# Seven-product blocks over six k-tiles, and a down projection in three parts, in a decoder layer on one core

## The chip, the core and the metric

The kernel runs on one core of one Trainium2 chip. The metric is the device time of one execution in microseconds (us), taken as the median of several. The engines are named as in the profile: PE does the matmuls (PEld the loading of its stationary operand), ACT and DVE the elementwise work, POOL a few small operations, and SP issues nearly all DMAs.

## The reference

One layer for 256 tokens of width 2048, all in float32:

```
x = x + 0.5 * SwiGLU_1(rmsnorm(x))          # D_FF = 5632
x = x + mixer(rmsnorm(x))                   # w_in: 2048 -> 11776, attention and a gated MLP, two merges, w_out
x = x + 0.5 * SwiGLU_2(rmsnorm(x))
out = rmsnorm(x)
swiglu(x) = (silu(x @ w_gate) * (x @ w_up)) @ w_down
```

Nearly all of the work is products of 256 tokens with large weights, which are read once from memory.

## The kernel before

**Products.** A weight is taken in columns of 512 (a "gemm" of the program) and in k-tiles of 128 rows. Both operands are split into a high and a low part; a k-tile's product is three matmuls per 128 tokens (high by high, high by low, low by high), so 6 for the 256 tokens. The activations are the stationary operand, the weights stream through as 512 columns.

**Steps.** The list of steps sets the order of nearly everything (lay_out, lines 118 to 150). An "n" step is two k-tiles of one gemm, 12 matmuls. `ends` holds the position of a step's end in units of an n step. Work that follows a gemm (activation, transposition, residual) is put on a list of callbacks by such a position and is issued when the loop over steps gets there (lines 1112 to 1123).

**Quads.** In most pairs of neighbouring gemms, four k-tiles (two pairs) are multiplied as 2 x 2 blocks in Strassen's way: with blocks b11, b21, b12, b22 of the weights (k-tile of a pair by gemm) seven products p1 to p7 take the place of eight. Each is an "s" step, 2 x 3 = 6 matmuls, half a unit long. DVE forms the differences of weights first (prepare, line 222: t1 = b12 - b11, t3 = b12 - b22, t2 = b22 - t1, t4 = b21 - t2); the sums of the activations are made once per input (sums_of, line 319). ACT copies partial results between banks after p1, p6 and p7 (lines 306 to 311); DVE does so after p7 and p5 (lines 313, 315). OPEN and CLOSE say where the s steps stand: p1, p6, p7 before the last 5, 3 and 1 steps of the pair before, p5, p3, p2, p4 after the first 1, 3, 4, 5 of their own.

**Splits.** Every step's weights pass through split (line 235): ACT copies to the high part (wh, line 249), DVE subtracts it to get the low part (wl, line 250). There are four buffers of two k-tiles for each (LA = 3, so LA + 1). A step's split is issued four steps ahead, right after the products of the step that used the same buffer (advance, line 1087).

**Memory traffic.** Plain weights come in units of four k-tiles of 1 MB into three buffers (load_unit, line 167). The blocks of a quad come from load_block (line 211), 512 KB each, into a "home"; the next quad's block is asked for as soon as the split has read the old one (FREES, line 231). All this is issued on SP in program order.

**FFN.** Its hidden width is 11 columns of 512 (f = 0 to 10). Two halves: gate and up for f = 0 to 5, then the down product of these 24 k-tiles for four column groups c, added to x (residual, line 435); then f = 6 to 10 and 20 k-tiles. After up, DVE multiplies gate and up (line 507), transposes in 32 x 32 blocks, a DMA out and four back finish the transposition (turn, line 355), and ev splits the result into the h tiles (line 512). Quads of the kernel before: 13 in the first FFN, 15 in the second, 6 in the mixer.

Of the kernel before, what the change touches and what calls it, by code (L numbers as in the profile page):

```python
# [37 lines left out]
LA = 3  # L38
CS = (2, 0, 0)
CM = 2  # L40
RAWB = 3
# [4 lines left out]
def layer(ctx: ExitStack, tc: tile.TileContext, a, out):  # L46
# [63 lines left out]
    def gemm(w, c0, rows0, nk, lhs, post, group=(1, None), bank=None, quad=None):  # L110
        gemms.append(dict(w=w, c0=c0, rows0=rows0, nk=nk, lhs=lhs, post=post, group=group, bank=bank or mm_bank,
                          quad=quad, steps=0, begun=[False] * NT, left=[3 * nk] * NT))


    OPEN = ((5, "p1"), (3, "p6"), (1, "p7"))
    CLOSE = ((1, "p5"), (3, "p3"), (4, "p2"), (5, "p4"))

    def lay_out():
        i = 0
        while i < len(gemms):  # L120
            g = gemms[i]
            size, stage = g["group"]
            chunk = g["quad"] and g["quad"]["chunk"]
            order = [(p, q) for p in range(size) for q in range(gemms[i + p]["nk"] // 2)
                     if not g["quad"] or q // 2 != chunk]
# [3 lines left out]
            if g["quad"]:  # L129
                quad = g["quad"]  # L130
                quad["gemms"] = gemms[i], gemms[i + 1]
                for k, form in OPEN:
                    steps.insert(len(steps) - k, ("s", (quad, form)))
                for k, form in reversed(CLOSE):
                    new.insert(k, ("s", (quad, form)))
                quads.append(quad)
                for h in quad["gemms"]:
                    h["left"] = [3 * (h["nk"] - 4) + 6] * NT
                gemms[i + 1]["left"][1] += 18
            steps.extend(new)  # L140
            i += size
        t = -1.0
        for kind, s in steps:
            t += 1 if kind == "n" else 0.5
            ends.append(t)
            if kind == "n":
                hus.append(s)
                s[0]["steps"] += 1
            else:
                s[0]["gemms"][s[1] in ("p3", "p5", "p6", "p7", "p1")]["steps"] += 1  # L150

# [15 lines left out]
    def load_unit(i, parts=(0, 4)):  # L167
        if i not in raws and RAWB <= i < 2 * RAWB:
            if i == RAWB:
                raws["more"] = big.tile([P, RAWB * UK, NC], F32, tag="A", name="more")  # L170
            raws[i] = raws["more"][:, (i - RAWB) * UK:(i - RAWB + 1) * UK]
# [23 lines left out]
    def gate_home():  # L195
        b_ = big.tile([P, 6, 2, NC], F32, tag="B", name="quads")
        return [b_[:, b] for b in range(6)] + [big.tile([P, NC], F32, tag="k2", name="part")]

    def merge_home():
        l_ = sb.tile([P, 3, 2, NC], F32, tag="L", name="quads")  # L200
        k = big.tile([P, 2, NC], F32, tag="k2", name="quads4")
        w = sb.tile([P, 3, NC], F32, tag="W", name="part")
        t = sb.tile([P, 2, NC], F32, tag="tmp", bufs=2, name="sum")
        return [l_[:, b] for b in range(3)] + [k, t, w[:, 1:3], w[:, 0]]

    def move_in(home):
        home["room"] = home["make"]()
# [3 lines left out]
    def load_block(quad, b):  # L211
        if quad is None:
            return
        g, j = quad["gemms"][b // 2], b % 2
        k0 = g["rows0"] + 4 * quad["chunk"] * P
        src = g["w"][k0:k0 + 4 * P, g["c0"]:g["c0"] + NC].rearrange("(q j p) c -> p j q c", p=P, j=2)
        SP.dma_start(blocks_of(quad)[b], src[:, j])

    def blocks_of(quad):
        return quad["home"]["room"]  # L220
# [10 lines left out]
    FREES = {"p1": 0, "p2": 1, "p7": 2, "p3": 3}  # L231

    place = {}

    def split(i, k=slice(0, 2)):
# [8 lines left out]
        if i not in splits:  # L244
            wh = big.tile([P, 2, NC], F32R, tag="wh", bufs=LA + 1, name=f"wh{i}")
            wl = big.tile([P, 2, NC], F32R, tag="wl", bufs=LA + 1, name=f"wl{i}")
            splits[i] = (wh, wl)
        wh, wl = splits[i]
# [6 lines left out]
    def product(g, t, act, w, last=False):  # L255
# [10 lines left out]
    def products(i, ts=range(NT), jjs=range(2), high_first=False):  # L266
# [10 lines left out]
        for jj in jjs:  # L277
            k = u * UK + 2 * j + jj
# [8 lines left out]
    def quad_products(i, quad, form):  # L287
# [6 lines left out]
        k = 4 * quad["chunk"]  # L294
        for q in range(2):
            if form in ("p1", "p2", "p4"):
                kk, tt = {"p1": (0, 0), "p2": (1, 0), "p4": (1, 1)}[form]
                hi, lo = (v[:, k + 2 * q + kk, tt * P:(tt + 1) * P] for v in first["lhs"]())
            else:
                hi, lo = (v[:, ("p5", "p6", "p7", "p3").index(form), q] for v in quad["forms"]())  # L300
            for act, w in ((hi, wh), (hi, wl), (lo, wh)):
                product(g, t, act, w[:, q], q == 1 and act is lo)
# [16 lines left out]
    def sums_of(i, store, v, name, tag="gate"):  # L319
# [3 lines left out]
        def sums():  # L323
            w = v.rearrange("p (q m) i b -> p m q i b", m=4)
            a0, a1, b0, b1 = (w[:, m] for m in range(4))
            got["f"] = f = sb.tile([P, 4, 2, P], F32, tag=tag, bufs=2, name=f"fs{name}")
# [6 lines left out]
        def parts():  # L333
            both = store()
            split_psum(both[:, 0], both[:, 1], got["f"])
# [4 lines left out]
    def forms_tile(pool, tag, name, keep):  # L340
        def store():
            keep["forms"] = pool.tile([P, 2, 4, 2, P], F32R, tag=tag, name=name)
            return keep["forms"]
        return store

    def forms_in(keep):
        return lambda: (keep["forms"][:, 0], keep["forms"][:, 1])
# [51 lines left out]
    def norm_open(n):  # L399
        xT["hi"] = big.tile([P, KD, S], F32R, tag="xhi", name=f"xhi{n}")  # L400
# [54 lines left out]
    def turn_x(i, n, c, lag, read=3):  # L455
        def evac(src):
# [4 lines left out]
            split_psum(hi, lo, src)  # L461
            if c == CS[n]:
                sums_of(i + lag, forms_tile(big, "oT", f"fx{n}", xT), src, f"x{n}")
# [7 lines left out]
    merge = dict(make=merge_home)  # L471

    def ffn(wg, wu, wd, down_post, group):
        halves = ((0, 6), (6, 11))
        home = dict(make=ffn_home)
        homes.append(home)
        for hf, (f0, f1) in enumerate(halves):
            st = {}

            def lhs_x():  # L480
                return xT["hi"], xT["lo"]

            def lhs_h(st=st):
                return st["hi"], st["lo"]

            for f in range(f0, f1):
# [10 lines left out]
                def post_up(e, banks, st=st, f=f, f0=f0):  # L497
                    sg = st["sg"]
                    kl = 4 * (f - f0)
                    if f == f0:  # L500
                        st["hi"] = big.tile([P, 24, S], F32R, tag="A", name=f"hhi{e}")
                        st["lo"] = big.tile([P, 24, S], F32R, tag="B", name=f"hlo{e}")
# [7 lines left out]
                    def ev(src):  # L510
                        hi, lo = st["hi"][:, kl:kl + 4], st["lo"][:, kl:kl + 4]
                        split_psum(turned(hi), turned(lo), src)
                        if f == f0:
                            sums_of(e + 10, forms_tile(sb, "L", f"fh{e}", st), src, f"h{e}")

                    at(e + 1, mul)
                    turn(e + 2, f"h{e}", 8, put_tokens(lambda: sg), lambda: flat(sg), ev)
# [8 lines left out]
                quad = dict(chunk=CS[n], forms=forms_in(xT), home=home if f or not n else merge)  # L526
                gemm(wg, f * NC, 0, KD, lhs_x, post_gate, BOTH if f else PAIR, bank, quad)
                gemm(wu, f * NC, 0, KD, lhs_x, post_up, BOTH, bank, quad)
            for c in range(4):
                if c % 2 == 0:  # L530
                    bank = side()
                    quad = dict(chunk=0, forms=forms_in(st), home=home)
                gemm(wd, c * NC, f0 * NC, 4 * (f1 - f0), lhs_h,
                     lambda e, banks, c=c, hf=hf: down_post(e, c, banks, hf == 1), PAIR if c == 0 else BOTH,
                     bank, quad)
# [60 lines left out]
    def post_gelu(key, j):  # L596
        def post(e, banks):
            if j == 0 and key == "vs":
                    uv = big.tile([P, 2, NT, SGW], F32, tag="A", name="uv")
                    mix["vs"], mix["u"] = uv[:, 0], uv[:, 1]  # L600
# [577 lines left out]
```

## Time and profile before

| | |
|---|---|
| median of 3 runs | 2014.4 us (2014.35 to 2016.39) |
| profiled execution: its own time | 2016.67 us |
| profiled execution: span from first to last instruction | 2014.9 us |
| mean granted PE clock | 0.998 |
| matmuls of products of weights (line 257) | 9108 of 9281 PE instructions |
| splits on DVE and on ACT (lines 250, 249), 128x1024 | 875 each |
| DMA | 471.54 MB, mean 234 GB/s |

The profile is one execution. A row of a group of instructions reads: line, engine, operation, tiles written <- read, shape written <- read, count, busy time in us, mean of one in ns, and idle time of that engine just before them with what ended it. In the order of time a row is start in us, duration in us, engine and instruction; [..] is the idle time before and its releaser. Matmuls overlap: one takes 0.38 us from start to end, but they start closer together than that.

### The profile page before, as it was taken

Reading aid. Unit: us, or ns where it says so; the run is one execution under the profiler, and the core shown is the slowest. Engines: PE = TensorE matmul, PEld = TensorE weight load, DVE = VectorE, ACT = ScalarE, POOL = GpSimd, SP = SyncE. Lnnn points to the kernel's source line nnn. Section 1 sums busy time; section 2 is a strip of 40 time slices with the busy share of each in tenths; the row PEclk is TensorE's granted clock in tenths of the full one; section 3 lists DMA queues with packets and bytes.
Section 4 is the critical chain, followed back from the end, with each engine's and each line's share of the span. In section 5 each row is a group of like instructions: output and inputs, shape, how many; then the busy total and the mean of one; then the engine's idle time right before and its main releaser. Section 6 shows DMA issues by size and latency. Waiting matters only on the chain.

```text
span 2014.9 us, 24165 instructions
## 1 busy us (share of the span) xinstructions
PE 1996.0 (99%) x9281; PEld 1741.1 (86%) x9281; DVE 1505.2 (75%) x1536; ACT 1141.1 (57%) x1286; POOL 11.2 (1%) x19
## 2 busy tenths in 40 slices
PE   9999999999999999999999999999999999999998
PEld 8888888888888888888888888878888888888887
DVE  6787866788877688675665777788878776787775
ACT  6556554555556566454554555566655554566554
POOL 0000000000000000000000000000000000000000
PEclk9999999999999999999999999999999999999999
DMA  9877776667775985888877666678777766677764
GB/s 314 271 246 243 232 238 204 209 217 236 247 245 167 317 272 169 240 287 251 262 244 239 225 202 224 222 245 255 228 234 241 243 208 201 220 243 230 233 214 143
DMA packets 249723, 471.54 MB, mean 234 GB/s; under 512 B 12684, under 2 KB 41224, under 8 KB 249480
## 3 DMA queue, kind: packets, MB, share of 16 engines
q1 hardware_dynamic: 249288, 469.47, 71.9%
q8 instruction: 72, 1.18, 0.2%
q10 hardware_dynamic: 320, 0.53, 0.1%
q14 instruction: 43, 0.35, 0.1%
HBM read 440.30 MB, written 29.66 MB: 233 GB/s over the span
## 4 chain that ended last, share of the span: by engine, by line
PE 87%; DMA 5%; DVE 4%; ACT 2%; issue 2%; SPq 1%; POOLq 0%; POOL 0%; ACTq 0%; DVEq 0%
PE qd L257 67%; PE mm L257 18%; DMA xt<-bmx 2%; DVE wl L250 2%; ACT wh L249 1%; DMA bmx<-btx 1%; DMA uroom<-bmu 1%; ACT xt L459 1%; DMA raw<-in_w_in_dram 1%; DMA p<-bmp 1%; SPq L368 1%; DVE btx L378 0%; ACT junk L406 0%; ACT xhi L350 0%; DVE xlo L351 0%
## 5 line engine op out<-in xcount | busy, mean ns | idle before, releaser
L250 DVE TENSOR_TENSOR wl<-raw,wh 128x1024 fp32r<-128x1024 f32 (+1 forms) x637 | 772.4, 1217 | 313.3 <-ACT wh L249 311.6
L249 ACT ACTIVATE wh<-raw 128x1024 fp32r<-128x1024 f32 (+1 forms) x637 | 666.5, 1051 | 503.7 <-PE qd L257 314.6
L257 PE MATMUL qd<-wl,xhi 128*128 128x512 f32 x1296 | 491.4, 379 | 0.7 <-DVE wl L250 0.7
L257 PE MATMUL qd<-wh,xhi 128*128 128x512 f32 x1296 | 491.2, 379 | 0.0
L257 PE MATMUL qd<-wh,xlo 128*128 128x512 f32 x1296 | 491.2, 379 | 0.0
L257 PEld LDWEIGHTS qd<-wl,xhi 128*128 128x128 f32 x1296 | 244.9, 189 | 36.3 <-DVE wl L250 1.6
L257 PEld LDWEIGHTS qd<-wh,xhi 128*128 128x128 f32 x1296 | 244.9, 189 | 34.9
L257 PEld LDWEIGHTS qd<-wh,xlo 128*128 128x128 f32 x1296 | 244.9, 189 | 34.6
L249 ACT ACTIVATE wh<-quads 128x1024 fp32r<-128x1024 f32 x142 | 149.9, 1056 | 182.7 <-PE qd L257 170.5
L257 PE MATMUL mm<-wh,xhi 128*128 128x512 f32 x608 | 231.1, 380 | 0.2 <-ACT xhi L432 0.2
L257 PE MATMUL mm<-wh,xlo 128*128 128x512 f32 x608 | 230.5, 379 | 0.0
L257 PE MATMUL mm<-wl,xhi 128*128 128x512 f32 x608 | 228.8, 380 | 0.6 <-DVE wl L250 0.4
L250 DVE TENSOR_TENSOR wl<-quads,wh 128x1024 fp32r<-128x1024 f32 x142 | 174.0, 1225 | 69.3 <-ACT wh L249 68.4
L257 PEld LDWEIGHTS mm<-wl,xhi 128*128 128x128 f32 x608 | 114.9, 189 | 17.9 <-DVE wl L250 1.8
L257 PEld LDWEIGHTS mm<-wh,xlo 128*128 128x128 f32 x608 | 114.9, 189 | 16.5 <-DVE xlo L433 0.3
L257 PEld LDWEIGHTS mm<-wh,xhi 128*128 128x128 f32 x608 | 114.9, 189 | 16.3 <-ACT xhi L432 0.3
L257 PE MATMUL qd<-wh,fx 128*128 128x512 f32 x352 | 119.3, 380 | 1.7 <-ACT wh L249 1.2
L250 DVE TENSOR_TENSOR wl<-sum,wh 128x1024 fp32r<-128x1024 f32 x64 | 78.4, 1224 | 44.5 <-ACT wh L249 42.6
L249 ACT ACTIVATE wh<-sum 128x1024 fp32r<-128x1024 f32 x64 | 67.7, 1057 | 34.8 <-PE qd L257 20.1
L257 PEld LDWEIGHTS qd<-wh,fx 128*128 128x128 f32 x352 | 66.5, 189 | 12.2 <-ACT wh L249 1.6
L257 PE MATMUL qd<-wl,fx 128*128 128x512 f32 x176 | 66.8, 380 | 0.0
L257 PE MATMUL qd<-wh,hhi23.0_663 128*128 128x512 f32 x172 | 65.2, 379 | 0.0
(410 smaller groups left out, 2474.2 us busy)
## 6 DMA issues: line engine op xcount, KB each, us to landing
raw<-in_w_in_dram SPq DMA_DIRECT2D x84, 1024.0 KB, 6.0
raw<-in_ffn_w_down_dram SPq DMA_DIRECT2D x72, 1024.0 KB, 5.1
raw<-in_ffn_w_gate_dram SPq DMA_DIRECT2D x65, 1024.0 KB, 5.9
raw<-in_ffn_w_up_dram SPq DMA_DIRECT2D x65, 1024.0 KB, 5.8
quads<-in_ffn_w_gate_dram SPq DMA_DIRECT2D x40, 512.0 KB, 5.2
quads<-in_ffn_w_up_dram SPq DMA_DIRECT2D x40, 512.0 KB, 3.7
quads<-in_ffn_w_down_dram SPq DMA_DIRECT2D x32, 512.0 KB, 3.8
raw<-in_w_sg_out_dram SPq DMA_DIRECT2D x12, 1024.0 KB, 6.0
```

Of the source, the lines that this page charges most:

```text
L249: ACT.activation(wh[:, k], r[:, k], AF.Copy)
L250: DVE.tensor_tensor(wl[:, k], r[:, k], wh[:, k].bitcast(F32), op=OP.subtract)
L257: PE.matmul(g["ps"][t], act, in_turn(w), start=not g["begun"][t], stop=g["left"][t] == 0, skip_group_check=g["quad"] is not None)
L368: SP.dma_start(e[32 * j:32 * j + 32].rearrange("p (i r) -> p i r", i=4), m[j])
L459: ACT.activation(v, v, AF.Copy, scale=g)
```

## The change

1. Quads have a number of k-tile pairs, nq. In the gate and up products (but f = 0 of the second FFN; f = 0 and 1 of the first have no quads, as before) and in the first part of down nq is 3: six k-tiles, seven products of 9 matmuls, steps of 0.75 unit; blocks of 768 KB, differences and splits of 1536 columns. Elsewhere nq stays 2.
2. Down is done in three parts, h blocks f = 0 to 3, 4 to 6 and 7 to 10 (16, 12 and 16 k-tiles). Gate and up run f = 0 to 3, then down 1, 4 to 7, down 2, 8 to 10, down 3. The h tiles hold four blocks ("rooms") in place of six.
3. The splits' buffers are one ring of 8 k-tiles for wh and one for wl. A step takes 2 or 3 neighbouring tiles; one that would pass the end begins at 0. A split is issued when its place overlaps no step whose products are still to be issued (has_room).
4. The block b11 and t1 share a place, so that b11's next load comes after p5's split and not after p1's. The order of closing forms is p5, p4, p3, p2, after 1, 2, 3 and 4 steps; the openings stand before the last 5, 3, 1 steps, or 4, 2, 1 where the pair before has fewer than ten plain steps. t1 and t2 are formed two steps and one step ahead of p6, t3 one after it, t4 five after it.
5. The last h block of a part turns in 6 units (2 until it is read back) rather than 8 (3), a unit earlier. The first loads of the first home come at 16 rather than 12. In the mixer several tiles change places (new tag E), with the same work.

The diff's core:

```
+RING = 8
+GATES = ((0, 4), (4, 8), (8, 11))
+PARTS = (dict(f=range(0, 4), rooms=(0, 1, 2, 3), k0=0, nq=3), dict(f=range(4, 7), rooms=(0, 1, 2), k0=0, nq=2),
+         dict(f=range(7, 11), rooms=(3, 0, 1, 2), k0=4, nq=2))
...
-    OPEN = ((5, "p1"), (3, "p6"), (1, "p7"))
-    CLOSE = ((1, "p5"), (3, "p3"), (4, "p2"), (5, "p4"))
+    CLOSE = ((1, "p5"), (2, "p4"), (3, "p3"), (4, "p2"))
+    def opening(count):
+        return zip((5, 3, 1) if count > 9 else (4, 2, 1), ("p1", "p6", "p7"))
...
+            width = 2 if kind == "n" else s[0]["nq"]
+            t += 1 if kind == "n" else width / 4
             ends.append(t)
+            if pos + width > RING:
+                pos = 0
+            slots.append((pos, pos + width))
+            pos += width
...
+    def has_room(k, i):
+        return all(slots[j][1] <= slots[k][0] or slots[k][1] <= slots[j][0] for j in range(i + 1, k))
...
-    def ffn_home():
-        c = big.tile([P, 4, 2, NC], F32, tag="C", name="quads")
-        k = big.tile([P, 2, NC], F32, tag="k2", name="sum")
-        w = sb.tile([P, 3, NC], F32, tag="W", name="part")
-        return [c[:, b] for b in range(4)] + [k, w[:, 1:3], w[:, 0]]
+    def ffn_home(home):
+        home["h"] = [big.tile([P, 16, S], F32R, tag=tag, name=f"h{tag}") for tag in "AB"]
+        c, e = (big.tile([P, 4096], F32, tag=tag, name="quads") for tag in "CE")
+        w = sb.tile([P, SGW], F32, tag="W", name="sum")
+        b11, b21, b12, b22, t2 = (v.rearrange("p (q c) -> p q c", q=3)
+                                  for v in (c[:, 0:SGW], c[:, SGW:2 * SGW], e[:, 0:SGW], e[:, SGW:2 * SGW], w))
+        return b11, b21, b12, b22, t2, b11, e[:, 2 * SGW:2 * SGW + NC]
...
-    FREES = {"p1": 0, "p2": 1, "p7": 2, "p3": 3}
+    FREES = {"p5": 0, "p2": 1, "p7": 2, "p3": 3}
...
+    ring = [big.tile([P, RING, NC], F32R, name=name) for name in ("wh", "wl")]
...
-            wh = big.tile([P, 2, NC], F32R, tag="wh", bufs=LA + 1, name=f"wh{i}")
-            wl = big.tile([P, 2, NC], F32R, tag="wl", bufs=LA + 1, name=f"wl{i}")
+        splits[i] = wh, wl = [v[:, slots[i][0]:slots[i][1]] for v in ring]
         ACT.activation(wh[:, k], r[:, k], AF.Copy)
         DVE.tensor_tensor(wl[:, k], r[:, k], wh[:, k].bitcast(F32), op=OP.subtract)
...
-        for q in range(2):
+        for q in range(quad["nq"]):
...
             if c == CS[n]:
-                sums_of(i + lag, forms_tile(big, "oT", f"fx{n}", xT), src, f"x{n}")
+                sums_of(i + lag, xT, 0, 2, forms_tile(big, "oT", f"fx{n}", 2), src, f"x{n}", tag)
+            elif n != 1 and c == CS[n] + 1:
+                sums_of(i + lag, xT, 2, 1, forms_tile(big, "k2", f"fy{n}", 1), src, f"y{n}", tag)
...
-            for k, what in ((-5, "t1"), (-4, "t3"), (-2, "t2"), (5, "t4")):
+            for k, what in ((-2, "t1"), (-1, "t2"), (1, "t3"), (5, "t4")):
                 prepared.setdefault(i + k, []).append((s[0], what))
...
-        while done < min(n, to):
+        while done < min(n, i + LA + min(i - 1, 2)) and has_room(done, i):
```

More of the change, by code (lines that the diff above doesn't have):

```diff
@@ L122, in lay_out @@
             size, stage = g["group"]
-            chunk = g["quad"] and g["quad"]["chunk"]
-            order = [(p, q) for p in range(size) for q in range(gemms[i + p]["nk"] // 2)
-                     if not g["quad"] or q // 2 != chunk]
+            quad = g["quad"]
+            taken = range(quad["k0"] // 2, quad["k0"] // 2 + quad["nq"]) if quad else ()
+            order = [(p, q) for p in range(size) for q in range(gemms[i + p]["nk"] // 2) if q not in taken]
             if stage:
@@ L128, in lay_out @@
             new = [("n", (gemms[i + p], q // 2, q % 2)) for p, q in order]
-            if g["quad"]:
-                quad = g["quad"]
+            if quad:
+                nq = quad["nq"]
                 quad["gemms"] = gemms[i], gemms[i + 1]
-                for k, form in OPEN:
+                for k, form in opening(count):
                     steps.insert(len(steps) - k, ("s", (quad, form)))
@@ L713, in post @@
             if (key, gi) == ("q", 0):
[L714 to L716 removed]
+                parts = big.tile([P, 4, one], F32R, tag="E", name="qk0")
+                kept = xT["both"]
                 def keep():
[L719 to L720 removed]
+                    for new, old in zip(mix["fs"], kept):
+                        ACT.activation(new, old.bitcast(F32), AF.Copy)
+                    mix["forms"] = {q: [v[:, :, q] for v in mix["fs"]] for q in range(2)}
                 at(e + 4, keep)
```

168 lines of the change are left out of this document (86 added, 82 removed).

## The prediction

> **What bounds the kernel now.** I read the page's busy shares first, then the busy time by stretches, then who waited for whom.
>
> ```profile
> span 2014.9 us, 24165 instructions
> PE 1996.0 (99%) x9281; PEld 1741.1 (86%) x9281; DVE 1505.2 (75%) x1536; ACT 1141.1 (57%) x1286; POOL 11.2 (1%) x19
> ```
>
> ```profile
> 100.00:500.00 400.00, 400.00 (x1855) 350.18 (x1854) 309.75 (x292) 226.20 (x236) 3.08 (x5) 1.00 0.71 228
> ```
>
> The row of the stretch (time, then PE, PEld, DVE, ACT, POOL with counts, clock, DMA share, GB/s) lies wholly in the first FFN: 1855 matmuls in 400 us without a gap at full clock, so one 512-column matmul costs 400/1855 = 0.2156 us of the path. I call it u. DVE is busy 77% there.
>
> ```profile
> ACT wh L249 <- PE qd L257: 540.3, 484, 2.8
> DVE wl L250 <- ACT wh L249: 455.7, 475, 3.8
> ...
> PE qd L257 <- DVE wl L250: 4.6, 4, 3.1
> ```
>
> These rows of the waits (total, times, longest) give the direction: the splits wait for PE to free a buffer, and PE hardly ever waits for a split. PE alone bounds the FFNs, because the splits run ahead of it. How far ahead is what the change touches.
>
> **What it saves.** A quad of two k-tile pairs takes 7 forms x 2 x 3 = 42 matmuls in place of 48 and saves 6; one of three pairs takes 63 in place of 72 and saves 9. Before: 13 quads in FFN 1, 15 in FFN 2 and 6 in the mixer, 34 x 6 = 204 saved. After: of three pairs 9 gate/up and 2 down in FFN 1, 10 and 2 in FFN 2, 23 in all; of two pairs 1 gate/up, 4 + 4 down and 6 in the mixer, 15. That saves 23 x 9 + 15 x 6 = 297. So 93 matmuls go, 93 x 0.2156 = **20.1 us**, all of it path. [...]
>
> **What the splits then cost.** The rows by shape (count, busy us, mean ns):
>
> ```profile
> L250 DVE TENSOR_TENSOR wl<-quads,wh 128x1024 fp32r<-128x1024 f32 x142 | 174.0, 1225 | 69.3 <-ACT wh L249 68.4
> L250 DVE TENSOR_TENSOR wl<-raw,wh 128x512 fp32r<-128x512 f32 x6 | 4.0, 692 | 1.3 <-ACT wh L249 1.3
> L225 DVE TENSOR_TENSOR quads<-quads 128x1024 f32<-128x1024 f32 x35 | 42.6, 1218 | 0.0
> L249 ACT ACTIVATE wh<-quads 128x1024 fp32r<-128x1024 f32 x142 | 149.9, 1056 | 182.7 <-PE qd L257 170.5 <-PE mm L257 9.6 <-DVE wl L250 1.5
> L249 ACT ACTIVATE wh<-raw 128x512 fp32r<-128x512 f32 x6 | 3.8, 633 | 2.2 <-DMA raw<-in_ffn_w_gate_dram 2.1
> ```
>
> 512 more columns cost DVE 0.53 us and ACT 0.42 us, so at 1536 columns I take DVE 1.76 us (split or block difference, line 225) and ACT 1.48 us. The page does not show that width; below 1.22 us it cannot be, and above 1.92 (0.692 + 1.225) two instructions would do it. Now the delays between the engines, from the order of time (start, us):
>
> ```profile
> 249.38 1.22 DVE L225 TENSOR_TENSOR sum<-quads,sum 128x1024 f32<-128x1024 f32 x1
> 250.52 1.22 DVE L250 TENSOR_TENSOR wl<-raw,wh 128x1024 fp32r<-128x1024 f32 x1
> ...
> 251.43 0.38 PE L257 MATMUL qd<-wh,xlo 128*128 128x512 f32 x1
> 251.84 1.06 ACT L249 ACTIVATE wh<-part 128x1024 fp32r<-128x1024 f32 x1 [1.53 <-PE qd L257]
> 252.93 1.23 DVE L250 TENSOR_TENSOR wl<-part,wh 128x1024 fp32r<-128x1024 f32 x1 [1.20 <-ACT wh L249]
> ```
>
> Two DVE instructions with nothing to wait for overlap by 0.08 (249.38 + 1.22 against 250.52), so behind another one a split of 1024 costs 1.14 and one of 1536 1.68. ACT starts 0.20 after PE's turn at the last matmul ends (251.43 + 0.22 to 251.84), DVE 0.03 after ACT. And where PE does wait:
>
> ```profile
> 652.21 2.35 DVE L250 TENSOR_TENSOR wl<-raw,wh 128x1024 fp32r<-128x1024 f32 x2
> ...
> 653.48 0.48 PE L257 MATMUL qd<-wl,hhi157.0_3285 128*128 128x512 f32 x1 [0.58 <-DVE wl L250]
> 653.80 0.38 PE L257 MATMUL qd<-wh,hlo157.0_3286 128*128 128x512 f32 x1
> ```
>
> The first of those two splits ends at 653.43; the matmul follows 0.05 later and the next one comes after 0.32 in place of 0.22. A wait therefore costs its length + 0.15.
>
> Per quad of a gate/up pair the DVE gains 7 splits and 4 differences of +0.53 and loses 2 splits of 1.22: +3.4 us, in a period that shrinks from 186 u = 40.1 to 183 u = 39.5 us. From 77% (31.1 us) it goes to 34.5/39.5 = **87%**: no bound as a sum, but dense in places, and there the ring decides.
>
> Before, four equal buffers meant that a split could start when PE was through with the step four back: PE then held three steps. A ring of 8 tiles with steps of 2 and 3 tiles holds three: a split starts when the step three back is read, and PE holds two. Behind a waiting split stand, in program order, ACT's copies for p1, p6 and p7 and its activations, and on DVE all that belongs to the next steps. I follow the opening of a three-pair quad, p1 n n p6 n (n: 12 u = 2.59 us; three-pair form: 9 u = 1.94). "Lead" is how long the split is done before PE's second matmul of that step needs it.
> - p1: PE holds p2 and an n, 1.94 + 2.59 = 4.53; the split takes 0.20 + 1.48 + 0.03 + 1.76 = 3.47. Lead 4.53 - 3.47 + 0.22 = 1.28.
> - n1, behind difference t1: DVE 1.68 + 1.14 = 2.82 while PE does p1, 1.94. Lead 0.40.
> - n2, behind t2: 2.82 against 2.59. Lead 0.17.
> - p6 reads t2, which DVE finished 1.14 before n2's split ended: ACT's part is done 0.03 + 1.48 later, so 0.40 after n2's, and DVE's 1.76 behind it, at 2.16. PE has 2.59. Lead 0.60.
> - n3, behind t3: 2.82 against 1.94. Lead -0.28: PE waits 0.28, and loses **about 0.4 us**.
>
> Before, the same stretch had two steps between t2 and p6, narrower differences, and one step more in PE's hands. With that, I count:
> - 23 such openings x 0.4 = 9.2 us.
> - In 9 of them, by the ring's own rule, p1 gets slot 0 to 3 and overlaps the step two back: PE then holds 6 u + 2.59 = 3.88, the lead at p1 is 0.63, n1 and n2 wait too (0.4 and 0.2): 9 x 0.65 = 5.9 us.
> - In 4, the first gate/up quad after each of the first two down parts of an FFN, a residual's two adds (below) fall in front of n3: 1.2 us each, 4.8.
> - In 5, the evacuation of an h block with the sums for its forms falls behind n3: 1.14 + 4 x 0.34 + the split 1.14 = 3.64 us against 2.59 + 0.15, so 0.9 + 0.15, and 0.2 at the next: 5 x 1.25 = 6.3.
>
> ```profile
> L440 DVE SCALAR_TENSOR_TENSOR x<-qd,x 128x512 f32<-128x512 f32 x32 | 20.5, 682 | 0.0
> L351 DVE TENSOR_TENSOR xlo<-xt,xhi 128x1024 fp32r<-128x1024 f32 x10 | 12.3, 1226 | 21.2 <-ACT xhi L350 21.2
> L331 DVE TENSOR_TENSOR fsx<-xt,fsx 128x256 f32<-128x256 f32 x3 | 1.3, 418 | 0.0
> ```
>
> That makes 26 us. The smaller things (the one-pair sums of x and h, four columns' residuals more per FFN, 16 x 0.68 us of DVE outside those places) I put at 0 to 8, taken as 5, from the nearest: 2 us of DVE each where the lead is thin. Waits: **31 us**, bounds 20 and 45, since 0.1 us more or less of lead at each of some 70 waits or near-waits is 7 us, and the width 1536 moves as much again.
>
> **What I cost at nothing.** The closing forms, n p5 n p4 n p3 n p2, take DVE 2.82 us a couple against PE's 4.53: 1.7 us of each is left for the product, the transposes and t4 that fall there; without it, 0.3 us a quad. The blocks (KB each, median us to landing):
>
> ```profile
> GB/s 314 271 246 243 232 238 204 209 217 236 247 245 167 317 272 169 240 287 251 262 244 239 225 202 224 222 245 255 228 234 241 243 208 201 220 243 230 233 214 143
> ...
> quads<-in_ffn_w_gate_dram SPq DMA_DIRECT2D x40, 512.0 KB, 5.2
> quads<-in_ffn_w_up_dram SPq DMA_DIRECT2D x40, 512.0 KB, 3.7
> ...
> xt<-bmx SPq DMA_DIRECT2D x40, 128.0 KB, 4.9
> ```
>
> A 768 KB block, at half as much again, lands in 8 us; b11, now freed at p5's split in place of p1's, is needed at p1's, after p5 n p4 n p3 n p2 n: 4 x 1.94 + 4 x 2.59 = 18 us. Raw loads queue behind it on SP as before. At the start of each FFN four blocks go at once, 3.1 MB in place of 2.1: 1 MB at 314 GB/s is 3.3 us, nothing if the raw buffers cover it, at most 6.6 for both. The last h block of a part turns in 6 units of 2.59 = 15.5 us from transpose to evacuation in place of 8, with its reads a unit earlier; two DMAs of about 5 us leave room, and if they didn't it would be a us or two, three times an FFN. Rooms, E and W tiles change places, not instructions; the mixer keeps its 6 quads of two pairs, and four steps still fit its ring.
>
> **The sum.** Against the profiled execution: 2014.9 us of span - 20.1 + 31 = 2025.8. Its own time is 2016.7, 1.8 above the span, and the median of the runs 2014.4; I apply the difference, +11, to the median: **2025 us**.
>
> **Rivals.**
> 1. *The ring still suffices; the 93 matmuls are simply gone.* For it: PE is 99% busy, DVE 75%, and it waited 4.6 us for DVE in all. [...] It decides if the lead at p1 is 0.3 us more than I count, or 1536 columns cost under 1.6 us. Against: the chain above uses measured delays only, and its lead ends below zero. Time 2014.4 - 20.1 = 1994; with half the waits, 2010. Chance 0.18 for this end (under 2010).
> 2. *Waits eat just the gain.* The openings and the five evacuations stay, the nine wraps and the rest vanish: 9.2 + 6.3 + 4.8 = 20. Time 2014. Chance 0.15.
> 3. *Slower by more: release by whole steps.* If a slot that overlaps one tile of the step two back waits for all of it, PE holds only one n, 2.59 us, for a split of 3.47: about 0.7 + 0.15 us in each of the 43 steps so placed (counted by the ring's rule), less the waits already there: some 25 us more, 2050. Against: PE's reads and the splits' writes are per tile in the code. Chance 0.07, with late DMAs beside it.
> 4. The forecast: chance 0.60.
>
> **How the numbers follow.** The forecast's own range is 2014.4 - 20.1 + (20 to 45), 2014 to 2039; the range to hold 8 in 10 goes from half-covered waits to the foot of rival 3: 2001 to 2044. About 0.2% (4 us) is what a measurement of this kernel can tell from no change. Faster by more: rival 1, 0.18. Within: rival 2 without its edges and the low edge of the forecast, 0.15. Slower: 0.67.
>
> **What would show it.** Right: PE's instructions fall to 9188; splits 128x1536 of about 1.76 us on DVE and 1.48 on ACT; PE waiting for DVE's wl some 20 to 35 us in all, in many pieces of 0.2 to 1.5 us, first of all at the second matmul of the step after p6; DVE near 81% of the span (1505 + 23 x 11 x 0.53 for the widths, and the rest about even, over 2025), PE under 99%. Wrong: PE's wait for wl under 15 us; or a wait on DMA or on h; or mixer stretches that change by more than a few us.

## The result, and the profile after

The change makes the kernel slower: 2042.5 us (2040.15 to 2044.13, 4 runs) against 2014.4 (2013.51 to 2016.39), a ratio of 1.0137 with the 95% interval 1.0120 to 1.0155. That is +28 us where +11 was forecast. It lies inside the range, near its upper end.

The page after, its first lines:

```profile
span 2041.6 us, 24153 instructions
PE 1996.8 (98%) x9188; PEld 1721.4 (84%) x9188; DVE 1633.8 (80%) x1572; ACT 1171.8 (57%) x1270; POOL 15.3 (1%) x19
```

The 93 matmuls are gone (9281 to 9188) and yet the span is 26.7 us longer. PE still reads 98% busy, since that share hides where it waits. The count of matmuls in a stretch shows it. The busy time by stretches, after (start and end; length; then PE, PEld, DVE, ACT, POOL with counts; clock; DMA share; GB/s):

```profile
100.00:660.00 560.00, 547.45 (x2494) 470.13 (x2492) 480.64 (x417) 322.91 (x321) 6.36 (x5) 0.99 0.68 221
...
1300.00:1400.00 100.00, 91.34 (x394) 75.64 (x393) 77.60 (x83) 60.87 (x85) 0.69 (x1) 0.97 0.66 219
1400.00:2030.00 630.00, 619.57 (x2836) 532.53 (x2835) 543.12 (x475) 367.67 (x368) 0.19 (x1) 1.00 0.67 219
```

and the same stages before:

```profile
100.00:640.00 540.00, 539.51 (x2500) 472.04 (x2499) 418.61 (x396) 306.86 (x326) 3.08 (x5) 1.00 0.70 227
...
1290.00:1390.00 100.00, 95.23 (x430) 81.37 (x429) 81.85 (x87) 67.11 (x92) 0.69 (x1) 0.98 0.71 228
1390.00:2000.00 610.00, 610.00 (x2828) 534.17 (x2827) 471.33 (x448) 344.29 (x367) 0.00 (x0) 1.00 0.70 224
```

Length less count x 0.2156 (u, the time of one matmul where PE waits for nothing) is the time that PE lost:

| stage | before | after |
|---|---|---|
| first FFN | 540 - 2500 u = 1.0 | 560 - 2494 u = 22.3 |
| w_out and the start of the second FFN | 100 - 430 u = 7.3 | 100 - 394 u = 15.1 |
| second FFN | 610 - 2828 u = 0.3 | 630 - 2836 u = 18.6 |

So 47.4 us of new losses, less 20.1 us of matmuls, is +27.3, near the +26.7 of the spans. In the FFNs DVE is busy 480.64/560 = 86%, where 87% was worked out.

The waits after (total, times, longest):

```profile
ACT wh L268 <- PE qd L276: 422.9, 325, 3.3
...
PE qd L276 <- DVE wl L269: 30.5, 52, 2.6
```

ACT waits less for PE (540 before), and PE now waits for DVE 52 times (4 before): the splits no longer run ahead. The two new widths, in the rows by shape:

```profile
L269 DVE TENSOR_TENSOR wl<-quads,wh 128x1536 fp32r<-128x1536 f32 x115 | 201.9, 1756 | 99.5 <-ACT wh L268 98.4
L268 ACT ACTIVATE wh<-quads 128x1536 fp32r<-128x1536 f32 x115 | 170.2, 1480 | 144.1 <-PE qd L276 134.9 <-PE mm L276 5.4 <-DVE quads L247 3.8
```

One opening of a three-pair quad in the first FFN, in order of time. Line 268 makes the high splits, 247 the differences, 269 the low splits; 276 is PE. [..] counts from the end of the matmul before:

```profile
325.58 1.48 ACT L268 ACTIVATE wh<-quads 128x1536 fp32r<-128x1536 f32 x1 [2.75 <-PE qd L276]
...
328.89 1.76 DVE L247 TENSOR_TENSOR quads<-quads 128x1536 f32<-128x1536 f32 x1
...
329.26 0.38 PE L276 MATMUL qd<-wh,xhi 128*128 128x512 f32 x1
...
330.56 1.22 DVE L269 TENSOR_TENSOR wl<-raw,wh 128x1024 fp32r<-128x1024 f32 x1
...
331.21 0.38 PE L276 MATMUL qd<-wh,xhi 128*128 128x512 f32 x1
...
331.83 0.48 PE L276 MATMUL qd<-wl,xhi 128*128 128x512 f32 x1 [0.25 <-DVE wl L269]
...
332.15 0.38 PE L276 MATMUL qd<-wh,xlo 128*128 128x512 f32 x1
...
338.40 1.22 DVE L269 TENSOR_TENSOR wl<-raw,wh 128x1024 fp32r<-128x1024 f32 x1
...
339.06 0.38 PE L276 MATMUL qd<-wh,xhi 128*128 128x512 f32 x1
...
339.67 0.48 PE L276 MATMUL qd<-wl,xhi 128*128 128x512 f32 x1 [0.23 <-DVE wl L269]
...
342.14 1.22 DVE L269 TENSOR_TENSOR wl<-raw,wh 128x1024 fp32r<-128x1024 f32 x1
342.15 0.38 PE L276 MATMUL qd<-wh,xhi 128*128 128x512 f32 x1
...
343.41 0.48 PE L276 MATMUL qd<-wl,xhi 128*128 128x512 f32 x1 [0.88 <-DVE wl L269]
```

Each wait ends 0.05 us after a split on DVE: behind t1 (328.89), behind t3 (the split of 338.40), and behind an h block's evacuation with its sums (342.14). A wait costs more than its [..]: from 331.21 two matmuls further PE is at 332.15, 0.94 us in place of 0.43, so a wait of 0.25 cost 0.51. By that, the 52 waits of 30.5 us cost some 30.5 + 52 x 0.26 = 44 us (an estimate), which is how they go with 47.4 us lost.

One place looks different. In the first FFN's first down part, DVE and SP, then ACT and PE:

```profile
184.80 1.30 DVE L396 STREAM_TRANSPOSE bth63.75_1370<-sg56.5_1225 128x512 f32<-128x512 f32 x2
...
186.13 0.34 SPq L380 DMA_DIRECT2D bmh63.75_1373<-bth63.75_1370  x1
...
191.68 0.37 SPq L238 DMA_DIRECT2D quads<-in_ffn_w_down_dram  x1
192.14 2.84 SPq L386 DMA_DIRECT2D sg56.5_1225<-bmh63.75_1373  x4
...
201.29 1.06 ACT L368 ACTIVATE hA<-sg56.5_1225 128x1024 fp32r<-128x1024 f32 x1 [5.84 <-DMA sg56.5_1225<-bmh63.75_1373]
...
201.66 0.38 PE L276 MATMUL qd<-wh,hB 128*128 128x512 f32 x1
...
203.77 0.48 PE L276 MATMUL qd<-wh,hA 128*128 128x512 f32 x1 [1.73 <-ACT wh L268]
205.56 0.80 PE L276 MATMUL qd<-wl,hA 128*128 128x512 f32 x1 [1.31 <-DVE wl L269]
206.15 0.63 PE L276 MATMUL qd<-wh,hB 128*128 128x512 f32 x1
206.58 0.63 PE L276 MATMUL qd<-wh,hA 128*128 128x512 f32 x1
...
211.20 0.38 PE L276 MATMUL qd<-wh,hB 128*128 128x512 f32 x1
```

The shortened turn of the last h block goes out at 186.13. Its read-back is issued at 192.14, behind a block's load on SP that had waited for its split. ACT stands 5.84 us for it, with the next splits queued behind. PE then waits twice, and afterwards its matmuls start 0.43 us apart in place of 0.22. From 201.66 to 211.20 are 15 matmuls: 9.54 us in place of 15 u = 3.2, so PE loses 6.3 us here.

The other such place lies at the start of the second FFN, where ACT waits for the last quarter of x. One row of before, then two of after:

```profile
1367.03 1.71 ACT L459 ACTIVATE xt<-xt,gcols 128x256 f32<-128x256 f32 x4 [1.48 <-DMA xt<-bmx]
```

```profile
1381.49 1.71 ACT L478 ACTIVATE xt<-xt,gcols 128x256 f32<-128x256 f32 x4 [3.09 <-DMA xt<-bmx]
...
1388.40 0.53 PE L276 MATMUL qd<-wl,xhi 128*128 128x512 f32 x1 [2.63 <-DVE wl L269]
```

The eleven matmuls up to 1392.14 take 7.2 us in place of 2.4, so PE loses 4.8 us there. Before, ACT stood 1.48 us at the same turn of x, which the change leaves as it was, and PE lost nothing.

### The profile page after: what moved, and what is told of

The parts are those of the page before. It is cut to its first block, busy times and chain, and to the rows that moved or that the text cites. A ratio compares the mean times of both kernels' runs of the same rounds, so it can differ in the third digit from the quotient of the medians.

```text
span 2041.6 us, 24153 instructions
## 1 busy us (share of the span) xinstructions
PE 1996.8 (98%) x9188; PEld 1721.4 (84%) x9188; DVE 1633.8 (80%) x1572; ACT 1171.8 (57%) x1270; POOL 15.3 (1%) x19
## 4 chain that ended last, share of the span: by engine, by line
PE 75%; DVE 11%; ACT 4%; DMA 4%; issue 4%; SPq 1%; DVEq 0%; ACTq 0%; POOLq 0%; POOL 0%
PE qd L276 53%; PE mm L276 21%; DVE wl L269 5%; ACT wh L268 3%; DVE sum L247 2%; DMA xt<-bmx 1%; DVE quads L247 1%; DMA bmx<-btx 1%; SPq L386 1%; DMA quads<-in_ffn_w_down_dram 1%; ACT xt L478 1%; DVE hB L369 0%; DVE x L459 0%; DVE btx L396 0%; ACT xhi L368 0%
## 5 line engine op out<-in xcount | busy, mean ns | idle before, releaser
L269 DVE TENSOR_TENSOR wl<-raw,wh 128x1024 fp32r<-128x1024 f32 (+1 forms) x575 | 695.6, 1215 | 183.8 <-ACT wh L268 181.9
L268 ACT ACTIVATE wh<-raw 128x1024 fp32r<-128x1024 f32 (+1 forms) x575 | 599.4, 1047 | 386.2 <-PE qd L276 204.0
L269 DVE TENSOR_TENSOR wl<-quads,wh 128x1536 fp32r<-128x1536 f32 (+1 forms) x185 | 287.3, 1553 | 129.1 <-ACT wh L268 127.5
L268 ACT ACTIVATE wh<-quads 128x1536 fp32r<-128x1536 f32 (+1 forms) x185 | 244.0, 1319 | 189.2 <-PE qd L276 165.5
L276 PE MATMUL qd<-wl,hA 128*128 128x512 f32 x564 | 216.6, 384 | 9.1 <-DVE wl L269 9.1
L276 PE MATMUL qd<-wh,hA 128*128 128x512 f32 x564 | 215.0, 381 | 1.7 <-ACT wh L268 1.7
L276 PE MATMUL qd<-wh,hB 128*128 128x512 f32 x564 | 214.8, 381 | 0.0
L268 ACT ACTIVATE wh<-sum 128x1536 fp32r<-128x1536 f32 (+1 forms) x76 | 100.0, 1316 | 103.1 <-PE qd L276 52.6
L269 DVE TENSOR_TENSOR wl<-sum,wh 128x1536 fp32r<-128x1536 f32 (+1 forms) x76 | 117.3, 1543 | 30.8 <-ACT wh L268 30.0
L276 PEld LDWEIGHTS qd<-wl,hA 128*128 128x128 f32 x564 | 107.2, 190 | 29.4 <-DVE wl L269 14.4
L276 PEld LDWEIGHTS mm<-wl,xhi 128*128 128x128 f32 x608 | 114.9, 189 | 18.3 <-DVE wl L269 2.2
```

The source lines that it names most:

```text
L268: ACT.activation(wh[:, k], r[:, k], AF.Copy)
L269: DVE.tensor_tensor(wl[:, k], r[:, k], wh[:, k].bitcast(F32), op=OP.subtract)
L276: PE.matmul(g["ps"][t], act, in_turn(w), start=not g["begun"][t], stop=g["left"][t] == 0, skip_group_check=g["quad"] is not None)
```

## The experiments

My theory when the runs began was the **ring theory**: the ring holds one step less in PE's hands, and the denser, wider work on DVE eats the rest of the lead. Against it stood a **queue theory** (bigger blocks, b11's later load, the shorter turn: transfers come late) and a **three-part theory** (the added residuals and turns cost it). The kernel before, beside these runs, took 2014.7 to 2015.0 us.

**Rings of 8, 9 and 10 tiles.** Each further tile takes 4 KB a partition (2 KB of wh, 2 of wl). To free 8 KB, all three runs load the plain weights in halves, after the first units, into four buffers of 512 KB in place of three of 1 MB; the control keeps the ring of 8, the others have 9 and 10:

```
-            raws[i] = big.tile([P, UK, NC], F32, tag="raw", bufs=RAWB, name=f"raw{i}")
+    raw = big.tile([P, 8, NC], F32, name="raw")
...
+    def raw_of(m):
+        return raws[m // 2][:, 2 * (m % 2):2 * (m % 2) + 2] if m < 12 else raw[:, 2 * (m % 4):2 * (m % 4) + 2]
...
-RING = 8
+RING = 10
```

> The changed kernel with one thing altered: after the first six units the plain weights are loaded two k-tiles at a time (512 KB) into four half buffers (16 KB a partition) in place of three buffers of four k-tiles (24 KB). The ring stays at 8 tiles. This is the control for the two larger rings. Ring theory (the extra waits come from the ring holding one step less in PE's hands): no change beyond 5 us, 2038 to 2048 us, and PE's wait for DVE's wl stays near the 30 us of the changed kernel. Queue theory (the extra time comes from transfers, which stand behind bigger blocks and later waits on SP): smaller loads that are asked for sooner shift it clearly, by 5 to 15 us in either direction. Three-part theory (the added residuals and turns cost it): no change.

> As the control, with a ring of 9 tiles in place of 8. Ring theory: a three-wide step still holds off the step three back, since 2 + 3 + 2 + 3 tiles need 10; so no gain, within 4 us of the control (about 2043). If in its place every added tile gave the splits more lead, this run would be 8 to 15 us faster than the control. Queue and three-part theories: as the control.

> As the control, with a ring of 10 tiles: four steps of 2 and 3 tiles fit in it, so a split may start again when PE is through with the step four back. Ring theory: the waits at the openings and at the wraps go, some 25 to 33 us; 2010 to 2018 us; PE's wait for wl falls from 30 us to under 8; what stays are the two places where ACT waits for a DMA, some 10 us together, and the start. Queue theory: as the control, 2038 to 2048. Three-part theory: as the control.

| run | median, us | ratio to before (95%) |
|---|---|---|
| ring 8, half buffers | 2056.0 | 1.0199 (1.0182 to 1.0216) |
| ring 9 | 2065.4 | 1.0247 (1.0230 to 1.0263) |
| ring 10 | 2012.4 | 0.9982 (0.9973 to 0.9992) |

Two more tiles are worth 43.6 us against the control. The stretches of the control (the first FFN, then the second):

```profile
100.00:660.00 560.00, 546.72 (x2493) 469.25 (x2492) 481.44 (x417) 324.30 (x322) 6.36 (x5) 1.00 0.70 221
...
1410.00:2040.00 630.00, 619.02 (x2832) 531.85 (x2831) 542.39 (x469) 367.69 (x367) 0.00 (x0) 1.00 0.70 221
```

and of ring 10:

```profile
100.00:640.00 540.00, 538.63 (x2486) 468.69 (x2485) 475.83 (x412) 320.51 (x320) 3.85 (x5) 1.00 0.72 228
...
1390.00:2000.00 610.00, 608.69 (x2813) 530.80 (x2813) 534.43 (x473) 360.56 (x362) 0.55 (x1) 1.00 0.71 224
```

The FFNs lose 22.5 + 19.4 us with 8 tiles, as in the changed kernel, and 4.0 + 3.5 with 10, at the same widths and with the same three parts. That is the ring theory's result; the three-part theory falls, and so does the queue theory as the main cause, since both expected no gain from a larger ring. PE's wait for wl fell to 11.1 us, where under 8 was expected. Two more things missed. The control is 13.4 us slower than the changed kernel, which I had allowed for under the queue theory alone. It isn't in the FFNs, as the counts show. Some 10 us of it are in the mixer, where 640 us (670 to 1310) hold 2956 matmuls and in the changed kernel (660 to 1300) 3003. There ACT waits for the smaller loads, which is the likely cause. The control's row:

```profile
ACT wh L277 <- DMA raw<-in_w_in_dram: 83.2, 46, 6.8
```

In the changed kernel that wait came to 19.1 us. And ring 9 was to equal ring 8, but is 9.4 us slower. Its mean granted clock is 0.992 against 0.996, and (1 - clock) x span is 16.5 us against 8.2. So most of the 9.4 us (each of the two figures is good to 1 us) goes with a lowered clock, of which the last section shows a case. Why ring 9 piles them up I did not follow further.

**Lead and width apart.** Every quad back to two pairs, with the ring of 8 (four steps), and in a second run with a ring of 6 (three steps, the last two lines):

```
-                quad = dict(k0=4 * CS[n], nq=2 if late else 3, forms=xT, home=merge if late else home)
+                quad = dict(k0=4 * CS[n], nq=2, forms=xT, home=merge if late else home)
-PARTS = (dict(f=range(0, 4), rooms=(0, 1, 2, 3), k0=0, nq=3), dict(f=range(4, 7), rooms=(0, 1, 2), k0=0, nq=2),
+PARTS = (dict(f=range(0, 4), rooms=(0, 1, 2, 3), k0=0, nq=2), dict(f=range(4, 7), rooms=(0, 1, 2), k0=0, nq=2),
-RING = 8
+RING = 6
```

> The changed kernel with every quad of two pairs of k-tiles (four steps of two tiles fill the ring of 8 again); the three parts of down, the ring, the order of the closing forms, the differences' places and the shorter turn stay. 60 matmuls come back that the three-pair quads in gate, up and the first down part had saved: 228 saved in place of 297, so 69 matmuls x 0.2156 = 14.9 us more of PE's work than the changed kernel, 24 fewer matmuls than before (5.2 us). Ring theory: the waits at the openings go; 2014.4 - 5.2 + some 10 us of the two DMA waits and the closer differences = 2010 to 2022 us. Three-part theory: its residuals and turns are all there, so 2042.5 + 14.9 = 2057 us less little. Queue theory: blocks are 512 KB again, but the later load of b11 and the shorter turn stay: 2025 to 2045.

> The run with every quad of two pairs, but with a ring of 6 tiles: three steps of two tiles, so the step of lead is gone again while every split and difference stays 1024 wide. Tells lead and width apart. If the loss of one step is enough by itself: 45 us or so over the run with two pairs and 8 tiles, 2055 to 2065 us. If it takes both (the dense 1536-wide work and the lost step), the estimate by the chain of leads is some 9 us in each FFN and a few in the mixer: 2015 + 18 = 2033 us, 2025 to 2045. If lead hardly matters and width does: under 2022 us.

With four steps 2015.2 us (ratio 1.0001, 0.9991 to 1.0010), with three 2048.5 (1.0165, 1.0150 to 1.0181). In the second run the last four steps, which the program keeps back for the end, don't fit into six tiles: one is overwritten, so the last columns are computed from other weights, and the last few us of that run are not read here. The FFN stretches with four steps:

```profile
100.00:650.00 550.00, 548.46 (x2540) 479.43 (x2539) 449.61 (x433) 320.36 (x343) 3.80 (x5) 1.00 0.71 228
1390.00:2000.00 610.00, 610.00 (x2828) 534.14 (x2827) 497.39 (x481) 354.57 (x380) 0.00 (x0) 1.00 0.70 224
```

and with three:

```profile
100.00:650.00 550.00, 545.60 (x2520) 474.81 (x2518) 448.74 (x429) 317.41 (x339) 5.80 (x5) 1.00 0.71 226
...
1410.00:2020.00 610.00, 605.13 (x2795) 526.93 (x2794) 495.46 (x474) 352.43 (x375) 0.00 (x0) 1.00 0.70 225
```

Time that PE lost in the two FFNs together, from these rows and those above:

| | four steps in the ring | three |
|---|---|---|
| two pairs (1024 wide) | 2.4 + 0.3 = 2.7 | 6.7 + 7.4 = 14.1 |
| three pairs (1536 wide) | 4.0 + 3.5 = 7.5 | 22.3 + 18.6 = 40.9 |

(The cell of three pairs with four steps has the half buffers; their control lost 41.9 us in the FFNs, so they don't touch it.) The run with two pairs and four steps keeps all of the three parts and stands at 2015 us, where the ring theory put it at 2010 to 2022, the three-part theory at 2057 and the queue theory at 2025 to 2045. The lost step by itself costs 11.4 us and the width by itself 4.8, but both together 38.2. Neither half of my theory explains the result alone. The estimate for the run with three steps, 2033, was too low by 15 us. Its FFNs cost 11.4 us where I allowed 18, and the other 22 of the 33 us over the run with four steps lie in other stages, for which I had allowed a few.

**The read-backs.** Both places where ACT waits for one, a unit later:

```
-                    turn(t_, f"h{e}", 8, put_tokens(lambda: sg), lambda: flat(sg), ev, 6 if last else 8,
+                    turn(t_, f"h{e}", 8, put_tokens(lambda: sg), lambda: flat(sg), ev, 7 if last else 8,
-        turn_x(e + (6 if c == 1 else 2), n, c, 6)
+        turn_x(e + (6 if c == 1 else 2), n, c, 7 if (n, c) == (2, 3) else 6)
```

> The changed kernel with one edit: the last h block of each part, and the last quarter of x ahead of the second FFN, are taken out of their turns one unit (2.59 us) later: 7 in place of 6 units. These are the two places where ACT waits for a read-back with splits queued behind it (5.8 us around 201 us, 3.1 us around 1381 us in the changed kernel's trace). Queue theory: those waits go, 6 to 10 us faster, 2032 to 2037. Ring theory: they are a part of late splits as much as a cause, and one unit later the evacuation's DVE work lands elsewhere in the same dense stretch: 0 to 5 us faster, 2037 to 2043.

2036.3 us (1.0108, 1.0094 to 1.0122), 6.2 us faster than the change: inside what the queue theory expected, at its slow edge. So on the short ring these two waits are worth some 6 of the 28 us; the other 22 this edit doesn't touch. They aren't a cause apart from the ring: x's turn is the same in the kernel before, where PE lost nothing by it, and with the ring of 10 ACT still stands 3.2 us for the same h block, while PE loses 4.0 us in that whole FFN. PE's wait for DVE's wl stays where it was (30.5 us, 56 times). Two stages of this run:

```profile
100.00:660.00 560.00, 548.14 (x2507) 470.55 (x2506) 484.43 (x421) 325.94 (x324) 6.39 (x5) 1.00 0.69 223
1300.00:1400.00 100.00, 92.12 (x413) 76.72 (x412) 81.56 (x87) 65.38 (x89) 0.69 (x1) 1.00 0.71 237
```

In these stretches the first FFN wins 13 matmuls' time (2.8 us) and the start of the second 19 (4.1 us). The granted clock of these stretches goes from 0.99 and 0.97 to 1.00. Behind the two read-backs it was 0.79, 0.50 and 0.86 by 4 us from 202 to 214 us, and 0.59 and 0.98 from 1388 to 1396, in the changed kernel; here it is 1.00 from 202 to 214 and from 1388 to 1392. By (1 - clock) x length that is 3.4 + 1.7 = 5.1 us of the 11.1 that PE lost at the two places (an estimate).

**The same kernel with the ring of 10, made better.** First blocks of a home one after another, and evacuations a unit later (the h edit above, and x for all quarters):

```
-        at(after, lambda home=home: move_in(home))
+        for k in range(4):
+            at(after + gap * k, lambda home=home, k=k: move_in(home, (k,)))
-        turn_x(e + (6 if c == 1 else 2), n, c, 6)
+        turn_x(e + (6 if c == 1 else 2), n, c, 7)
```

> The run with half buffers and a ring of 10 tiles, with the four first blocks of each home asked for one after another (1 unit apart in the first FFN, 2 in the mixer and the second FFN) in place of all at once. In the mixer's first 35 us the run with ring 10 lost some 5 us to late plain loads which stood behind those 2 MB. Ring theory: that is what is left to get: 2004 to 2010 us, against 2012. If the order of these loads does not matter: 2012.

> As the run with ring 10 and the spread first blocks, with the evacuation of the last h block of a part and of all x quarters ahead of the mixer and of the second FFN a unit later (7 in place of 6), since ACT runs a step further ahead with ring 10 and waits longer there (17 us in all for the x read-backs). Ring theory: 2 to 5 us faster than without it, 2000 to 2008 us. If those waits are covered by the lead: the same within 2 us.

> Half buffers, ring of 10, the evacuations a unit later, and the first blocks of each home asked for at once as in the changed kernel. The spread by itself cost 6 us (a first quad waited for its own blocks), so without it: 1996 to 2003 us, against 2002.9 with both. If the later evacuations worked only because the loads were spread: 2008 to 2013.

> As the one before, with the first blocks asked for one unit apart in every home. Between all at once and two units apart: plain loads are late by less, and the first quad's blocks are there in time. 1997 to 2002 us if both effects are real; equal to the one before within 2 us if neither matters beside the later evacuations.

| ring 10, half buffers | median, us | ratio (95%) |
|---|---|---|
| as it is | 2012.4 | 0.9982 (0.9973 to 0.9992) |
| spread, 2 apart | 2018.3 | 1.0019 (1.0011 to 1.0028) |
| spread and later | 2002.9 | 0.9944 (0.9931 to 0.9956) |
| later alone | 2001.5 | 0.9942 (0.9928 to 0.9956) |
| later, 1 apart | 2003.6 | 0.9945 (0.9932 to 0.9958) |

The spread was wrong: it costs 5.9 us by itself and brings nothing beside the later evacuations. These are worth 10.9 us (2012.4 to 2001.5), more than the 2 to 5 I gave them. The three with later evacuations are within each other's intervals. Of the best one, later alone, two stages:

```profile
100.00:640.00 540.00, 539.02 (x2491) 469.69 (x2489) 476.40 (x415) 320.73 (x320) 3.87 (x5) 1.00 0.73 229
...
1390.00:1990.00 600.00, 599.18 (x2773) 523.08 (x2772) 526.39 (x465) 355.61 (x358) 0.55 (x1) 1.00 0.71 225
```

2.9 + 2.1 us are lost in the FFNs, with DVE at 88% in both. Before, it was 1.3 us. So of the 20.1 us of matmuls that the change removes most are a gain in the FFNs where the lead is kept. The whole run, 2001.5 us, is 0.58% (0.44 to 0.72) faster than the kernel before and 41 us faster than the changed one. How much of the 0.58% is the change's own isn't shown: later evacuations were not tried in the kernel before, and without them the ring of 10 is only 0.2% faster.

**Less work on DVE.** The differences t3 and t4 on POOL, in the changed kernel and in the best one:

```
-        DVE.tensor_tensor(out, x, y, op=OP.subtract)
+        (POOL if what in ("t3", "t4") else DVE).tensor_tensor(out, x, y, op=OP.subtract)
```

> The changed kernel (ring of 8) with the differences t3 and t4 formed by POOL, which is busy 15 us in all, in place of DVE. Takes 2 x 1.75 us of DVE work out of each three-pair quad, t3 right out of the stretch after p6 where the lead ended below zero (0.28 us short behind t3's 1.68 us). Ring theory with dense work: if POOL forms a difference in under some 4 us and leaves DVE alone, the second matmul after p6 waits no more: 23 x 0.5 us and a part of the rest, 10 to 18 us faster, 2025 to 2033. If POOL is slower than that, p7's split waits for t3 in place of it: 2040 to 2060 or more. If DVE's load has nothing to do with the waits: 2042.

> Ring of 10 and the evacuations a unit later, with t3 and t4 formed by POOL. With four steps in the ring the splits have lead enough, so taking 3.5 us a quad from DVE should bring little: within 4 us of the run without it (1996 to 2006). If POOL's differences are late, or slow DVE while they run, slower by 5 us or more.

2174.3 us (1.0787, 1.0770 to 1.0804) and 2069.2 (1.0269, 1.0254 to 1.0284): 132 and 68 us slower than without. The expectations named two dangers, that POOL is slow and, for the second run, that it slows DVE; the trace of the first run shows both: POOL took 4.31 us for t3, where DVE takes 1.75, and DVE's t2 beside it 4.87. Rows by shape, in the changed kernel with POOL:

```profile
L247 DVE TENSOR_TENSOR sum<-quads 128x1536 f32<-128x1536 f32 x23 | 111.9, 4865 | 0.0
L247 POOL TENSOR_TENSOR quads<-quads 128x1536 f32<-128x1536 f32 x23 | 99.2, 4313 | 684.1 <-DVE quads L247 684.1
```

and one pair of them in order of time:

```profile
360.63 4.36 POOL L247 TENSOR_TENSOR quads<-quads 128x1536 f32<-128x1536 f32 x1 [32.92 <-DVE quads L247]
...
361.60 5.00 DVE L247 TENSOR_TENSOR sum<-quads 128x1536 f32<-128x1536 f32 x1
```

POOL's t3 starts as soon as t1 is done, beside DVE's t2, and t2 takes 4.87 us in place of 1.75. So DVE, which was to be relieved, is held up. These runs say nothing of what less work on DVE alone would bring.

## Why the prediction was right in direction and wrong in size

- **What it saves**, 93 matmuls and 20.1 us: right. PE's count is 9188, and where PE waits for nothing a matmul still takes 0.2157 us (610/2828, with two pairs and four steps).
- **The widths**, 1.76 and 1.48 us: right (1.756, 1.480).
- **The ring holds one step less**: right, and with the wider work the cause. With the step given back at the same widths the FFNs' losses fall from 41.9 to 7.5 us; with two pairs the same lost step costs 11.4.
- **The opening followed step by step**: right. The opening shown is one of the nine whose p1 begins at slot 0: ACT starts its split at 325.58, 0.20 after PE frees the place, and p1's first matmul is at 329.26, so PE held 329.26 - 325.38 = 3.88 us, as was worked out for these nine. Behind t1 the second matmul was to wait 0.25 us: its turn was 331.21 + 0.22 and the split ended at 331.78, 0.35 late. Behind t3 the split was to be 0.28 late and was 0.34; the evacuation with sums 0.9, and it was 0.99. Summed over the three-pair openings by PE's starts in the trace (start to start less u, step by step): behind t3 10.8 us (9.2 forecast), the wraps 5.3 (5.9), the residuals 5.0 (4.8), the evacuations and sums before p7 9.9 (6.3). The two openings that hold ACT's two stalls are not in these sums.
- **The waits, 31 us: the term that came out wrong.** It stood for all that the splits cost, bounds 20 to 45, and it measured 47.4. Of that the place at 201 us is 6.3 and the start of the second FFN 7.8. The remaining 33.3 (21.3 + 18.3 - 6.3), all in the FFNs, is the kind that was counted, 2 us from the forecast.
- **The step that failed: the read-backs, costed at nothing.** For the shortened turn I had written that two DMAs of about 5 us leave room in 15.5 us, and that it would be "a us or two" if they didn't; for x's turn I had no term. PE lost 6.3 and 4.8 us there. I counted to where PE needs the block, but ACT comes to the evacuation while PE is still behind: it stood from 195.45 (201.29 - 5.84), 10.65 us after the transposition began. And I took the DMAs' own times and not SP's queue, where the read-back stood until 192.14 behind a block's load. Then every split behind ACT is late, and with a step less of lead that reaches PE: I had followed that lead at the openings, and not at these two places. The 768 KB blocks landed in 4.5 to 6.9 us (medians), where 8 was worked out, and no split waited for one.
- **"A wait costs its length + 0.15"**: right for the time by which a split is late, but not for the [..] of the rows, where it is 0.26 more, since these count from the end of the matmul before. And it failed at three places: behind 1.73 and 1.31 us of waiting, and behind 2.19 and 2.63 (last section), the matmuls came 0.43 us apart; these stretches, at a granted clock of 0.50 in the first, are a term that no line of the prediction has.
- **The rivals.** "The ring still suffices" (1994 us) is false with 8 tiles; with 10 and the later evacuations the change comes nearest to it, 2001.5. The busy shares, PE's 99% and DVE's 75%, led to it; the page of the changed kernel has PE at 98% with 47 us of new losses. Release by whole steps (2050) would have come near the time, but the openings came out at the lengths of the other chain: ACT had its place at 325.58, 3.88 us ahead, and not 2.59.
- **The signs named in advance**: PE's 9188, the widths, DVE at 80% (81 forecast), PE's wait for wl of 30.5 us (20 to 35) came true. Of the signs against, the wait on DMA and on h came true as well, and the stage with w_out lost 7.8 us more. That the time fell inside the range is in part luck: its upper end was drawn for the release by whole steps, with late DMAs only beside it, and the read-backs took the time there.

Open: what the 3 us are that the start of the second FFN lost beside x's read-back. With two pairs and four steps the same stage (1290 to 1390, 413 matmuls) still loses 11.0 us in place of 7.3, so they don't seem to need the short ring. Whether the ring of 10 with 1 MB loads would be faster still is open too; no run has both.

## What to carry to other kernels

Where a fast engine is fed through a ring, count how many steps it holds while the next is made, and do so again when steps grow wider: here, in the FFNs, the lost step cost 11 us, the width 5, and both 38. When the bound engine reads 98% busy, count its instructions per stretch against its best rate before believing that it never waits. Count a transfer's slack from where its queue lets it be issued (here 192.14 us, behind a block's load) to where the engine that reads it comes to it (ACT at 195.45, while PE still worked without a wait up to 201.66). While ACT stood 5.84 us for it, the next splits stood behind it, and PE lost 6.3 us.

## What the runs showed of the hardware

**The clock fell behind some of PE's waits.** In the changed kernel's trace it did so behind two waits of 1.73 and 1.31 us with a single matmul between. By stretches of 4 us (PE's busy time and count, clock, DMA share, GB/s):

```profile
202.00:206.00 4.00, 0.96 (x3) 0.79 0.39 153
206.00:210.00 4.00, 4.00 (x11) 0.50 0.07 10
210.00:214.00 4.00, 4.00 (x17) 0.86 0.76 252
```

Three matmuls in 4 us, then 4 us at a granted clock of 0.50 with 11 matmuls in place of 18.5. In the same trace the matmuls also start 0.43 us apart behind two single waits, of 2.19 us (at 1333.62) and of 2.63 us (at 1388.40, granted clock 0.59 from 1388 to 1392). It didn't follow every wait: behind six single ones of 1.29 to 1.64 us (the longest at 258.84) they start 0.22 us apart from the second on. In the run with a ring of 9, waits of 0.97 and 1.31 us with one matmul between stand before 347.36; behind them the matmuls start 0.43 us apart, at a granted clock of 0.72 from 348 to 352 us. What sets the clock back isn't shown.

**DVE took longer beside POOL.** In the pair of rows above POOL ends at 360.63 + 4.36 = 364.99, and DVE's operation, started at 361.60, ends at 366.60: 1.61 us later, about the 1.75 us that it takes in the changed kernel, where DVE forms t3 itself. So it looks as if it had stood until POOL was done; the cause isn't shown. Over the run t2 took 4.87 us on average at 1536 columns in place of 1.75, and 3.17 at 1024 in place of 1.22.
